# Attention scores by pairs of heads on partition halves, with one copy of k, in a Trainium2 encoder layer

## The chip, the cores and the metric

The kernel runs on one core of one Trainium2 chip. The metric is the device time in microseconds (us) of one execution, lower is better. The kernel before takes 1902.78 us, the median of 3 runs (1901.52 to 1905.02).

Five engines work from queues of their own: PE (TensorE, the matrix engine, whose weight loads the profile lists apart as PEld), DVE (VectorE), ACT (ScalarE), POOL (GpSimd) and SP (SyncE, which here only issues transfers). Each takes its instructions in the order of its queue, and waits on semaphores for the others.

## What is computed

The reference is one encoder layer, applied to two sequences of 1024 positions of width 1024 (16 tiles of 128 positions in all). Cut to the part that the change touches:

```python
def windowed_gqa(q, k, v, q_gain, k_gain, sink, rel_table):   # 8 heads of 64, 2 kv heads, GROUP = 4
    q = rms_norm(q.reshape(B, S, N_KV, GROUP, HEAD_DIM), q_gain)
    k = rms_norm(k.reshape(B, S, N_KV, HEAD_DIM), k_gain)
    ...                                     # kband, vband: the 3 blocks of 128 keys around a block of queries
    scores = jnp.einsum("bnqkgd,bnskd->bnkgqs", qb, kband).astype(jnp.float32)
    scores = scores * (1.0 / math.sqrt(HEAD_DIM))
    scores = jnp.where(mask[None, :, None, None], scores + bias[None, None], NEG)
    m = jnp.maximum(jnp.max(scores, axis=-1, keepdims=True), s_sink)
    e = jnp.exp(scores - m)
    probs = e / (jnp.sum(e, axis=-1, keepdims=True) + jnp.exp(s_sink - m))
    out = jnp.einsum("bnkgqs,bnskd->bnqkgd", probs.astype(v.dtype), vband)

def encoder_layer(...):
    h = rms_norm(x, norm1); proj = h @ w_in           # q, k, v and the gMLP halves gu, gv
    a = rms_norm(windowed_gqa(q, k, v, ...), attn_out_gain)
    g = rms_norm(chunked_spatial_gating(gu, gv, v_gain, w_s, b_s), gmlp_out_gain)
    x = x + jnp.concatenate([a, g], axis=-1) @ w_o
    h2 = rms_norm(x, norm2)
    return x + (jax.nn.silu(h2 @ w_gate) * (h2 @ w_up)) @ w_down
```

Query heads 0 to 3 use kv head 0, heads 4 to 7 use kv head 1. The inputs and outputs are float32.

## The kernel before

**Precision.** Each product is made from a high and a low part of both operands: high by high, high by low and low by high, three matmuls that add up in one PSUM bank (`mm3`, lines 221 to 225). ACT writes the high part of an operand, DVE the low part (the operand minus its high part).

**Stages.** The program loads and splits weights and makes the projections of tiles 0 to 3. Then comes the attention stage: for each of the 16 tiles, projection, normalisation of q and k, scores, softmax, product with v. After it come the gMLP part, the output projection, and the feed-forward part, which takes up most of the span.

**One tile in the attention stage**, by the names of the code:

- `proj_pieces` and `proj_evac` (lines 321 to 351): 24 matmuls of 512 columns make q (`pq`), 24 of 256 columns make k and v (`pkv`); ACT writes them to `qk` and `v`.
- `qk_sum`, `qk_scale` (353 to 373): DVE sums squares by head, POOL takes the power -1/2 (`qk_r`), and DVE multiplies. k is scaled by an instruction of its own (line 366), which also writes each of the two k heads twice, side by side; q is scaled by line 373.
- `qk_turn` (375 to 383): PE transposes two blocks of k (`pk`, one for each kv head, its two copies giving the two partition halves) and four of q (`pt`, two heads each).
- `qk_hi`, `qk_lo` (385 to 410): ACT writes the high parts, two of k (line 389) and two of q (394, each on 64 partitions); DVE the low parts, two of k (402) and two of q (408). In `qt` a head has its high part on its own partition half and its low part on the other half, and k stands on both halves of its tile.
- `Attn.scores(h)` (424 to 444): with that layout two matmuls over 128 rows do the work of a head (four partial products): `qt` by the high part of k, then by the low part. DVE then adds the bias and takes the minimum of a row (the signs are turned; line 435). Keys are 384 for 12 of the 16 tiles, and 256 for the first and last of each sequence. The results go to the four banks of the pool `xx`.
- `exps`, `norm`, `norm2` (446 to 475): ACT takes the exponentials, and DVE makes the factor of a row from the row's sum and the sink, with small instructions on 8 columns (lines 463 to 465, 471 to 475).
- `turn`, `turn_dma` (477 to 491): DVE or ACT writes the high half-precision part `ph` of the probabilities, POOL the low part (482), and SP issues one transposing transfer for a pair of heads into `pT`.
- `pv(h)` (493 to 504): nine matmuls of 64 columns for a head with 384 keys, into `po`.
- `finish`, `finish_pow`, `finish2` (506 to 523): DVE multiplies by the factor, ACT sums squares, POOL takes a power (`a_r`), DVE multiplies once more (line 522), and SP stores the tile.

**What sets the order.** A list of events gives each of these steps of each tile a time from the table `AT` (8 units to a tile), so that the projection of one tile, the scores of another and the product with v of a third are interleaved. The events are sorted and written out. The build's scheduler orders the queues from that, and POOL's queue is kept as written.

**Buffers.** Pools of 4 KB buffers in SBUF go by tags (line 87): 8 of tag M hold `sc`, `ph` and `pT`; 12 of tag L hold the k and v of both sequences (four k buffers and one of v for each) and `o`; 9 of tag S hold `qk`, `qt` and pieces of x.

Of the kernel before, what the change touches and what calls it, by code (L numbers as in the profile page):

```python
# [16 lines left out]
P = 128  # L17
# [3 lines left out]
TS = 8  # L21
# [7 lines left out]
NEG = -1e30  # L29
SQRT_2_PI = math.sqrt(2.0 / math.pi)  # L30
# [24 lines left out]
def kernel(  # L55
# [92 lines left out]
    nsk = cp.tile([P, NH], F32, name="nsk")  # L148
    nc.vector.tensor_scalar_mul(nsk, sks, -1.0)
# [155 lines left out]
    isv = cp.tile([P, 1], F32, name="isv")  # L305
    nc.gpsimd.tensor_tensor(sv, vtot, nhalf[:, :1], ALU.pow)
    nc.gpsimd.tensor_tensor(isv, vtot, pm[:, 1:2], ALU.pow)
    nc.vector.tensor_scalar_mul(sv, sv, 512.0)
    nc.vector.tensor_scalar_mul(isv, isv, 1.0 / 512.0)
# [4 lines left out]
    def seq_tiles(s):  # L314
        kT[s] = [[k4("L", f"k{c}{s}_{v}", (P, TS * P), F32R) for v in range(NKV)] for c in "hl"]
        vS[s] = k4("L", f"v{s}", (P, TS, 2, P), F16)
# [4 lines left out]
    def proj_pieces(t):  # L321
# [9 lines left out]
        nc.scalar.mul(qk[:, 0:AW], pq, r1)  # L331
# [31 lines left out]
    def qk_scale(t):  # L363
        qk, rqk = live[t]
        kd = qk[:, 640:896].rearrange("p (v c d) -> p v c d", v=NKV, c=2)
        nc.vector.tensor_tensor(
            kd,
            qk[:, AW : AW + P].rearrange("p (v d) -> p v d", v=NKV)[:, :, None, :].to_broadcast([P, NKV, 2, HD]),
            rqk[:, 8:10][:, :, None, None].to_broadcast([P, NKV, 2, HD]),
            ALU.mult,  # L370
        )
        qd = qk[:, 0:AW].rearrange("p (h d) -> p h d", h=NH)
        nc.vector.tensor_tensor(qd, qd, rqk[:, 0:8][:, :, None].to_broadcast([P, NH, HD]), ALU.mult)

    def qk_turn(t):
        qk = live[t][0]
        pk = mm(f"pk{t}", [P, NKV, P])
        for v in range(NKV):
            nc.tensor.transpose(pk[:, v, :], qk[:, 640 + v * P : 640 + (v + 1) * P], ident)
        pt = mm(f"pt{t}", [P, NH // 2, P])  # L380
        for j in range(NH // 2):
            nc.tensor.transpose(pt[:, j, :], qk[:, j * P : (j + 1) * P], ident)
        live[t] = (pk, pt)

    def qk_hi(t):
        s, i = divmod(t, TS)
        pk, pt = live[t]
        for v in range(NKV):
            nc.scalar.mul(kT[s][0][v][:, i * P : (i + 1) * P], pk[:, v, :], kgs)
        qt = k4("S", f"qt{t}", (P, NH, P), F32R)  # L390
        pairs = qt.rearrange("p (a b) t -> p a b t", b=2)
        for b in range(2):
            rows = slice(b * HD, b * HD + HD)
            nc.scalar.mul(pairs[rows, :, b, :], pt[rows], qg8[rows])
        qT[t] = qt

    def qk_lo(t):
        s, i = divmod(t, TS)
        pk, pt = live.pop(t)
        for v in range(NKV):  # L400
            ks = slice(i * P, (i + 1) * P)
            nc.vector.scalar_tensor_tensor(
                kT[s][1][v][:, ks], pk[:, v, :], kgs, kT[s][0][v][:, ks].bitcast(F32), ALU.mult, ALU.subtract
            )
        pairs = qT[t].rearrange("p (a b) t -> p a b t", b=2)
        for b in range(2):
            rows, other = slice(b * HD, b * HD + HD), slice((1 - b) * HD, (2 - b) * HD)
            nc.vector.scalar_tensor_tensor(
                pairs[other, :, b, :], pt[rows], qg8[rows], pairs[rows, :, b, :].bitcast(F32), ALU.mult, ALU.subtract
            )  # L410

    class Attn:
# [11 lines left out]
        def scores(self, h):  # L424
            t, W = self.t, self.W
            hp, j = divmod(h, 2)
            if j == 0:
                self.prs[hp] = k4("M", f"sc{t}_{hp}", (P, 2, 384))
            sc = self.prs[hp]
            v = h // 4  # L430
            ps = xx(f"ps{t}_{h}", [P, 384])
            keys = slice(self.lo_b * P, self.lo_b * P + W)
            nc.tensor.matmul(ps[:, :W], qT[t][:, h, :], kT[self.s][0][v][:, keys], start=True, stop=False)
# [1085 lines left out]
```

## Time and profile before

| | |
|---|---|
| median of the runs | 1902.78 us (1901.52 to 1905.02) |
| the profiled execution | 1903.98 us, its span 1902.2 us |
| first scores to last product with v | 56 to 317 us of the span |
| busy in the span: PE, DVE, ACT, POOL | 1827.1, 1251.1, 1027.5, 223.5 us |
| busy from 0 to 56 us: PE, DVE, ACT, POOL | 45.87, 29.77, 33.51, 17.82 us |
| busy from 310 us to the end: PE, DVE, ACT, POOL | 1558.86, 987.85, 793.89, 58.01 us of 1592.20 |

The profile is one execution, slightly slower than the median. "Busy" is the time in which an engine's instructions run; PE's matmuls overlap, and their ends are modelled, so the step from the start of one matmul to the start of the next tells more about PE than its busy time. A row of instruction groups reads: line, engine, operation, output and inputs by the names of the code, shapes, count, then busy time in us and mean length in ns, then the engine's idle time just before them with what ended it. PEclk is the granted share of TensorE's clock, and the DMA share the mean busy share of the 16 DMA engines.

### The profile page before, as it was taken

The page shows a single profiled execution, that of the slowest core. Times are in us where ns is not written, and L with a number is a line of the kernel's source. Part 1 is how long each engine was busy: PE and PEld are TensorE (multiplying, and loading weights), DVE is VectorE, ACT ScalarE, POOL GpSimd, SP SyncE. Part 2 cuts the span into 40 slices and gives each one's busy share as a digit, 9 for nine tenths or more (in the row PEclk, how much of TensorE's full clock was granted, in tenths as well). Part 3 has the DMA queues.
Part 4 walks back from the last instruction along what each step waited for, and adds up shares of the span by engine and source line. Part 5 has one row for each costly group of instructions (what it writes and reads, how often), then busy time and mean ns, then how long its engine had stood idle before and what let it go on. Part 6 is the DMA issues. An engine that isn't in the chain of part 4 may idle for free.

```text
span 1902.2 us, 26114 instructions
## 1 busy us (share of the span) xinstructions
PE 1827.1 (96%) x9584; PEld 1006.5 (53%) x9584; DVE 1251.1 (66%) x2321; ACT 1027.5 (54%) x1930; POOL 223.5 (12%) x214
## 2 busy tenths in 40 slices
PE   8789988999899999999999999999999999999999
PEld 6677766878655444444444444444444444444444
DVE  4989997688776778545555556456456855654661
ACT  6677887776566785544445345345344453333340
POOL 3366653111100000000000000000000000000000
PEclk9899989999999999999999999999999999999999
DMA  7478898443376886223223133133164564333641
GB/s 239 109 164 174 169 201 227 156 144 111 100 233 211 290 271 215 103 105 117 88 106 116 69 115 106 64 119 106 45 207 168 188 228 133 112 110 100 221 144 44
DMA packets 216209, 282.05 MB, mean 148 GB/s; under 512 B 103283, under 2 KB 138099, under 8 KB 216081
## 3 DMA queue, kind: packets, MB, share of 16 engines
q1 hardware_dynamic: 215632, 280.02, 48.3%
q8 instruction: 75, 1.23, 0.3%
q14 instruction: 54, 0.43, 0.1%
q0 software_dynamic: 304, 0.10, 0.0%
q10 hardware_dynamic: 144, 0.26, 0.0%
HBM read 177.04 MB, written 80.23 MB: 135 GB/s over the span
## 4 chain that ended last, share of the span: by engine, by line
PE 58%; DVE 2%; DMA 2%; issue 2%; ACT 1%; POOL 0%; POOLq 0%; SPq 0%; DVEq 0%
PE pd L1356 7%; PE pd L1358 7%; PE pd L1357 7%; PE pd L1082 4%; PE pd L1084 4%; PE pd L1083 4%; PE pa L1083 4%; PE pa L1082 4%; PE pa L1084 4%; PE pc L1082 4%; PE pc L1084 4%; PE pc L1083 4%; PE pb L1082 2%; PE pb L1083 2%; PE pb L1084 2%
## 5 line engine op out<-in xcount | busy, mean ns | idle before, releaser
L1356 PE MATMUL pd<-wop,a 128*128 128x512 f16 x616 | 233.5, 379 | 2.5 <-ACT a L117 2.5
L1357 PE MATMUL pd<-wop,a 128*128 128x512 f16 x616 | 233.5, 379 | 0.0
L1358 PE MATMUL pd<-wop,a 128*128 128x512 f16 x616 | 233.3, 379 | 0.0
L1083 PEld LDWEIGHTS <-op 128*128 128x128 f16 x1232 | 120.7, 98 | 149.2 <-issue 7.3
L1082 PEld LDWEIGHTS <-op 128*128 128x128 f16 x1232 | 122.5, 99 | 143.5 <-issue 1.0
L1084 PEld LDWEIGHTS <-op 128*128 128x128 f16 x1232 | 120.7, 98 | 146.8 <-issue 2.0
L1082 PE MATMUL pa<-top,op 128*128 128x512 f16 x352 | 133.4, 379 | 0.6 <-ACT ua L1200 0.6
L1084 PE MATMUL pa<-top,op 128*128 128x512 f16 x352 | 133.4, 379 | 0.0
L1083 PE MATMUL pa<-top,op 128*128 128x512 f16 x352 | 133.4, 379 | 0.0
L117 ACT ACTIVATE wop<-wd,wdr_r 128x512 f16<-128x512 f32 x66 | 47.3, 720 | 153.4 <-PE pd L1358 150.5
L117 ACT ACTIVATE a<-as,asr_r 128x512 f16<-128x512 f32 x154 | 102.2, 709 | 33.3 <-DMA as<-act_d 13.5
L482 POOL TENSOR_TENSOR ph<-sc,ph 128x768 f16<-128x768 f32 (+1 forms) x64 | 107.6, 1682 | 88.0 <-DVE ph L481 64.9
L118 DVE SCALAR_TENSOR_TENSOR wop<-wd,wdr_r,wop 128x512 f16<-128x512 f32 x66 | 49.2, 749 | 100.0 <-ACT wop L117 100.0
L118 DVE SCALAR_TENSOR_TENSOR a<-as,asr_r,a 128x512 f16<-128x512 f32 x154 | 108.8, 746 | 7.2 <-ACT a L117 6.9
L1211 ACT COPY ub<-pc 128x512 f32<-128x512 f32 x44 | 25.8, 585 | 160.0 <-PE pc L1084 160.0
L1356 PEld LDWEIGHTS <-a 128*128 128x128 f16 x616 | 60.4, 98 | 75.8 <-ACT a L117 3.4
L1358 PEld LDWEIGHTS <-a 128*128 128x128 f16 x616 | 60.3, 98 | 73.0 <-DVE a L118 0.7
L1357 PEld LDWEIGHTS <-a 128*128 128x128 f16 x616 | 60.3, 98 | 72.2
L451 ACT ACTIVATE sc<-sc,mx 128x384 f32<-128x384 f32 (+1 forms) x128 | 74.7, 584 | 26.4 <-DVE mx L435 25.6
L1025 ACT ACTIVATE junk_e<-g 128x1024 f32<-128x1024 f32 x44 | 46.4, 1054 | 75.9 <-DVE g L1195 75.9
L1217 DVE TENSOR_TENSOR ub<-ub,ua 128x512 f32<-128x512 f32 x44 | 30.4, 692 | 82.2 <-ACT ub L1211 82.2
L1192 ACT ACTIVATE g<-g,rs 128x512 f32<-128x512 f32 x57 | 41.1, 722 | 62.4 <-DVE g L1227 35.5
(381 smaller groups left out, 4806.9 us busy)
## 6 DMA issues: line engine op xcount, KB each, us to landing
as<-act_d SPq DMA_DIRECT2D x77, 512.0 KB, 3.7
act_d<-g SPq DMA_DIRECT2D x66, 256.0 KB, 2.0
xs<-in_xT_dram SPq DMA_DIRECT2D x28, 512.0 KB, 4.6
tr<-t_d SPq DMA_DIRECT2D x28, 512.0 KB, 5.4
raw<-in_wg_dram SPq DMA_DIRECT2D x24, 512.0 KB, 3.8
raw<-in_wu_dram SPq DMA_DIRECT2D x24, 512.0 KB, 4.2
act_d<-sa SPq DMA_DIRECT2D x44, 256.0 KB, 2.6
act_d<-sb SPq DMA_DIRECT2D x44, 256.0 KB, 2.9
```

Source lines behind the costliest of these rows:

```text
L117: nc.scalar.mul(hi, src, gain)
L118: nc.vector.scalar_tensor_tensor(lo, src, gain, hi, ALU.mult, ALU.subtract)
L451: nc.scalar.activation(sc[:, j, :W], sc[:, j, :W], AF.Exp, bias=self.mn[:, h : h + 1], scale=-1.0, accum_out=self.sums[:, h : h + 1],)
L482: nc.gpsimd.tensor_sub(ph[:, 1], sc[:, :, :W], ph[:, 0])
L1025: nc.scalar.activation(junk_e[0], src, AF.Square, accum_out=acc)
L1082: nc.tensor.matmul(ps, op[:, 0, k, :], th[:, k, :], start=first and k == 0, stop=False, **more)
L1083: nc.tensor.matmul(ps, op[:, 0, k, :], tl[:, k, :], start=False, stop=False, **more)
L1084: nc.tensor.matmul(ps, op[:, 1, k, :], th[:, k, :], start=False, stop=last and k == 3, **more)
L1192: nc.scalar.activation(dst, src, AF.Silu, scale=iv)
L1356: nc.tensor.matmul(ps, a[:, 0, s, cs], wop[:, 0], start=first and n == 0, stop=False, **kw)
L1357: nc.tensor.matmul(ps, a[:, 0, s, cs], wop[:, 1], start=False, stop=False, **kw)
L1358: nc.tensor.matmul(ps, a[:, 1, s, cs], wop[:, 0], start=False, stop=end, **kw)
```

## The change

Heads h and h+4, which have different kv heads, become a pair (`hp` from 0 to 3): head h on partitions 0 to 63, head h+4 on 64 to 127.

- q is written out of `pq` in the order of the pairs. k is scaled together with q by one DVE instruction, and is not copied; it is transposed once, both kv heads at a time, and its high and low parts are one instruction each. So are those of q, which are now two separate halves of `qt`.
- A pair's scores are six matmuls over 64 rows each, by turns on the lower and the upper partition half: three partial products (high by high, high by low, low by high) for each of the two heads. Both heads' scores are issued at one event, half a unit after the even head's and half a unit before the odd head's.
- The row factor takes two small DVE instructions in `norm` (for three) and two in `norm2` (for four); the scale of v goes into the constant that is added before the last normalisation.
- The last multiplication of a tile (`finish2`) goes from DVE to ACT.
- `pT` of every other pair lies in a buffer of tag L, where k's second copies (two buffers for each sequence) are no longer held.

```diff
     def qk_scale(t):
         qk, rqk = live[t]
-        kd = qk[:, 640:896].rearrange("p (v c d) -> p v c d", v=NKV, c=2)
-        nc.vector.tensor_tensor(
-            kd,
-            qk[:, AW : AW + P].rearrange("p (v d) -> p v d", v=NKV)[:, :, None, :].to_broadcast([P, NKV, 2, HD]),
-            rqk[:, 8:10][:, :, None, None].to_broadcast([P, NKV, 2, HD]),
-            ALU.mult,
-        )
-        qd = qk[:, 0:AW].rearrange("p (h d) -> p h d", h=NH)
-        nc.vector.tensor_tensor(qd, qd, rqk[:, 0:8][:, :, None].to_broadcast([P, NH, HD]), ALU.mult)
+        qd = qk[:, 0:640].rearrange("p (h d) -> p h d", d=HD)
+        nc.vector.tensor_tensor(qd, qd, rqk[:, :, None].to_broadcast([P, 10, HD]), ALU.mult)
...
     def qk_turn(t):
         qk = live[t][0]
-        pk = mm(f"pk{t}", [P, NKV, P])
-        for v in range(NKV):
-            nc.tensor.transpose(pk[:, v, :], qk[:, 640 + v * P : 640 + (v + 1) * P], ident)
+        pk = mm(f"pk{t}", [P, P])
+        nc.tensor.transpose(pk, qk[:, AW:640], ident)
...
     def qk_hi(t):
-        for v in range(NKV):
-            nc.scalar.mul(kT[s][0][v][:, i * P : (i + 1) * P], pk[:, v, :], kgs)
-        qt = k4("S", f"qt{t}", (P, NH, P), F32R)
...
+        nc.scalar.mul(kT[s][0][:, i * P : (i + 1) * P], pk, kgs)
+        qT[t] = k4("S", f"qt{t}", (P, 2, NH // 2, P), F32R)
+        nc.scalar.mul(qT[t][:, 0], pt, qg8)
...
     def qk_lo(t):
...
+        nc.vector.scalar_tensor_tensor(
+            kT[s][1][:, ks], pk, kgs, kT[s][0][:, ks].bitcast(F32), ALU.mult, ALU.subtract
+        )
+        nc.vector.scalar_tensor_tensor(
+            qT[t][:, 1], pt, qg8, qT[t][:, 0].bitcast(F32), ALU.mult, ALU.subtract
+        )
...
-        def scores(self, h):
+        def scores(self, hp):
...
-            nc.tensor.matmul(ps[:, :W], qT[t][:, h, :], kT[self.s][0][v][:, keys], start=True, stop=False)
-            nc.tensor.matmul(ps[:, :W], qT[t][:, h, :], kT[self.s][1][v][:, keys], start=False, stop=True)
...
+            ps = [xx(f"ps{t}_{hp}_{v}", [P, 384]) for v in range(NKV)]
+            for n, (a, b) in enumerate(((0, 0), (0, 1), (1, 0))):
+                for v in range(NKV):
+                    rows = slice(v * HD, (v + 1) * HD)
+                    nc.tensor.matmul(
+                        ps[v][:, :W], qT[t][rows, a, hp, :], kT[self.s][b][rows, keys], start=n == 0, stop=n == 2
+                    )
...
         def norm(self):
...
+            self.e = e = small("ab", NH)
+            nc.vector.tensor_tensor(e, self.mn, skc, ALU.min)
+            nc.vector.tensor_add(e, e, sks)
+            nc.scalar.activation(e, e, AF.Exp)
 
         def norm2(self):
...
+            self.f = small("f", NH)
+            nc.vector.tensor_add(self.e, self.sums, self.e)
+            nc.vector.reciprocal(self.f, self.e)
...
-            pT = k4("M", f"pT{self.t}_{hp}", (P, 2, 2, W), F16)
+            pT = k4("L" if hp % 2 else "M", f"pT{self.t}_{hp}", (P, 2, 2, W), F16)
...
         def finish_pow(self):
-            self.ra = rsqrt_mean("a", self.ms, 1, EPS, MIX_UP)
+            t = small("a_e", 1)
+            nc.vector.scalar_tensor_tensor(t, self.ms, MIX_UP**-2, epsv, ALU.mult, ALU.add)
+            self.ra = small("a_r", 1)
+            nc.gpsimd.tensor_tensor(self.ra, t, nhalf[:, :1], ALU.pow)
 
         def finish2(self):
             o = self.o
-            nc.vector.tensor_scalar_mul(o[:, 0], o[:, 0], self.ra)
+            nc.scalar.mul(o[:, 0], o[:, 0], self.ra)
...
         for h in range(NH):
-            at(T + A + h + AT["sc"], lambda t, h: att[t].scores(h), t, h)
-            at(T + A + 8 + h + AT["pv"], lambda t, h: att[t].pv(h), t, h)
+            at(T + A + 8 + h + AT["pv"], lambda t, h: att[t].pv(h % 2 * GROUP + h // 2), t, h)
             if h % 2:
+                at(T + A + h - 0.5 + AT["sc"], lambda t, h: att[t].scores(h // 2), t, h)
```

How the queues move shows at three places of tile 6. On PE before, a head's two score matmuls (`ps6_1` is the second head) stand alone between a product with v (`po4`) and pieces of a projection (`pq9`):

```order
L504 MATMUL po4_1783<-v0_417,pT4_3_1881 128x64
L433 MATMUL ps6_1_2027<-kh0_0_413,qt6_1620 128x384
L434 MATMUL ps6_1_2027<-kl0_0_415,qt6_1620 128x384
L223 MATMUL pq9_2014<-wq_hi_176,xh9_1776 128x512
L224 MATMUL pq9_2014<-wq_lo_177,xh9_1776 128x512
```

On PE of the change, the six of a pair (`ps6_1_0` and `ps6_1_1` are the two heads of pair 1) stand between pieces of the same projection:

```order
L226 MATMUL pq9_1990<-wq_hi_176,xl9_1772 128x512
L421 MATMUL ps6_1_0_2041<-kh0_414,qt6_1589 128x384
L421 MATMUL ps6_1_1_2042<-kh0_414,qt6_1589 128x384
L421 MATMUL ps6_1_0_2041<-kl0_415,qt6_1589 128x384
L421 MATMUL ps6_1_1_2042<-kl0_415,qt6_1589 128x384
L421 MATMUL ps6_1_0_2041<-kh0_414,qt6_1589 128x384
L421 MATMUL ps6_1_1_2042<-kh0_414,qt6_1589 128x384
L224 MATMUL pq9_1990<-wq_hi_176,xh9_1751 128x512
```

Two pairs of matmuls of two heads have become six in a row that change the partition half at each step. On DVE before, between the output of tile 4 (`o4`) and the last small instruction of its row factor (`f`):

```order
L508 TENSOR_TENSOR o4_2056<-po4_1783,f_1825 128x512
L435 ISA sc6_1_2051,mx_1991<-ps6_2_2052,bias_398 128x384
L435 ISA mx_1991 128x1
L471 TENSOR_TENSOR den_2079<-sums_1734,ab_1978 128x8
L366 TENSOR_TENSOR qk8_1891<-qk8_1891,qk_r_1989 128x256
L472 TENSOR_TENSOR den_2079<-den_2079,ab_1978 128x8
L156 TENSOR_SCALAR a_e_2069<-a_ms_2058 128x1
L373 TENSOR_TENSOR qk8_1891<-qk8_1891,qk_r_1989 128x512
L473 RECIPROCAL den_2079<-den_2079 128x8
L335 TENSOR_TENSOR rs_2152<-rstd_all_175,sv_407 128x1
L522 TENSOR_SCALAR o4_2056<-o4_2056,a_r_2071 128x512
L475 SCALAR_TENSOR_TENSOR f_2083<-ab_1978,isv_408,den_2079 128x8
```

On DVE of the change, at the same place:

```order
L493 TENSOR_TENSOR o4_2023<-po4_1758,f_1802 128x512
L459 TENSOR_TENSOR ab_1950<-sums_1707,ab_1950 128x8
L372 TENSOR_TENSOR qk8_1867<-qk8_1867,qk_r_1959 128x640
L460 RECIPROCAL f_2057<-ab_1950 128x8
L341 TENSOR_TENSOR rs_2125<-rstd_all_175,sv_407 128x1
L219 TENSOR_SCALAR x_e_2202<-x_ms_2072 128x1
L504 SCALAR_TENSOR_TENSOR a_e_2036<-a_ms_2025,epsv_408 128x1
```

The two scalings (lines 366 and 373) are one of 640 columns, two of the small instructions are gone, and the multiplication by `a_r` (line 522) has left the queue. It stands in ACT's queue now, as line 510, between the high part of k and that of q of tile 8:

```order
L442 ACTIVATE sc6_1_2040,sums_1962<-sc6_1_2040,mx_1961 128x384 x2
L386 ACTIVATE kh1_1450<-pk8_2079,kgs_91 128x128
L510 ACTIVATE o4_2023<-o4_2023,a_r_2038 128x512
L388 ACTIVATE qt8_2099<-pt8_2081,qg8_101 128x512
L333 ACTIVATE qk9_2122<-pq9_1990,rstd_all_175 128x2x4x64
```

POOL's queue has the same rows in the same order as before, but for one power at the start that is gone.

More of the change, by code (lines that the diff above doesn't have):

```diff
@@ L29 @@
 NEG = -1e30
+SINK_CLAMP = 80.0
 SQRT_2_PI = math.sqrt(2.0 / math.pi)
@@ L399, in qk_lo @@
         pk, pt = live.pop(t)
[L400 to L410, printed above, removed]
+        ks = slice(i * P, (i + 1) * P)
+        nc.vector.scalar_tensor_tensor(
[4 more added lines that the diff above has]
+        )
     class Attn:
```

77 lines of the change are left out of this document (31 added, 46 removed).

## The prediction

> **What bounds the kernel now.** I read the windows first, to find the stage that the change touches and the engine that is full there. The columns are the length, then the busy time of PE, PEld, DVE, ACT and POOL, the granted clock, the DMA share and GB/s:
>
> ```profile
> core 0: us, PE busy (x) PEld busy (x) DVE busy (x) ACT busy (x) POOL busy (x), PEclk, DMA share, GB/s
> 56.00:310.00 254.00, 222.34 (x1995) 178.47 (x1994) 233.50 (x616) 200.06 (x494) 147.63 (x102) 0.95 0.80 168
> ```
>
> In the attention stage DVE works for 233.50 of 254 us, 92%. PE's 222.34 holds the overlap of its matmuls; its own pace comes below. After 310 us nothing of attention is left but the last products with v, so whatever the stage gains or loses moves the end by as much. The next view is what PE waited for within the same window (total us, times, longest):
>
> ```profile
> PE ps L433 <- DVE mx L435: 7.4, 6, 2.3
> PE po L502 <- DMA pT<-ph: 6.3, 9, 1.4
> PE pk L379 <- DVE qk L366: 4.2, 4, 1.4
> PE pkv L223 <- DVE kl L402: 4.0, 5, 1.0
> PE pk L379 <- DVE den L472: 2.6, 2, 1.8
> PE pt L382 <- DVE rs L335: 2.3, 4, 0.8
> PE pk L379 <- DVE a_e L156: 1.9, 3, 1.3
> PE pt L382 <- DVE a_e L156: 1.0, 4, 0.3
> PE pt L382 <- DVE den L473: 1.0, 3, 0.4
> ...
> PE pt L382 <- DVE den L471: 0.2, 1, 0.2
> ```
>
> All but the DMA row name DVE: 7.4 + 4.2 + 4.0 + 2.6 + 2.3 + 1.9 + 1.0 + 1.0 + 0.2 = 24.6 us, and nearly all of these lines are ones that the change thins out. So the stage is bound by DVE, with PE close behind.
>
> **DVE.** The rows by shape, from 40 to 340 us (busy us, mean ns):
>
> ```profile
> L408 DVE SCALAR_TENSOR_TENSOR qt<-pt,qg,qt 64x512 fp32r<-64x512 f32 x32 | 24.0, 750 | 0.9
> L522 DVE TENSOR_SCALAR o<-o,a_r 128x512 f32<-128x512 f32 x16 | 21.9, 1371 | 4.5 <-POOL a_r L158 4.4
> L366 DVE TENSOR_TENSOR qk<-qk,qk_r 128x256 f32<-128x256 f32 x15 | 20.6, 1372 | 6.4 <-POOL qk_r L158 6.3
> L373 DVE TENSOR_TENSOR qk<-qk,qk_r 128x512 f32<-128x512 f32 x16 | 11.7, 734 | 0.0
> L402 DVE SCALAR_TENSOR_TENSOR kl<-pk,kgs,kh 128x128 fp32r<-128x128 f32 x32 | 9.7, 339 | 0.0
> L463 DVE TENSOR_TENSOR m<-mx,nsk 128x8 f32<-128x8 f32 x16 | 9.6, 600 | 0.0
> L464 DVE TENSOR_TENSOR ab<-m,mx 128x8 f32<-128x8 f32 x16 | 6.8, 424 | 0.0
> L475 DVE SCALAR_TENSOR_TENSOR f<-ab,isv,den 128x8 f32<-128x8 f32 x16 | 6.5, 406 | 0.0
> L472 DVE TENSOR_TENSOR den<-den,ab 128x8 f32<-128x8 f32 x16 | 4.5, 279 | 0.0
> ```
>
> Line 522 leaves DVE: 21.9 us. The low parts are half as many at the same length (512 and 128 columns on 128 partitions; a row's length does not tell 64 partitions from 128 here): 12.0 + 4.8 = 16.8. The small instructions 464, 472 and 475 go: 6.8 + 4.5 + 6.5 = 17.8.
>
> The two scalings become one of 640 columns. What it costs hangs on why line 366 takes 1372 ns for 256 columns where line 373 takes 734 for 512. The timeline tells:
>
> ```profile
> 86.95 1.64 POOL L482 TENSOR_TENSOR ph<-sc,ph 128x768 f16<-128x768 f32 x1
> 87.02 1.85 DVE L366 TENSOR_TENSOR qk<-qk,qk_r 128x256 f32<-128x256 f32 x1 [0.46 <-POOL qk_r L158]
> 88.87 0.68 DVE L373 TENSOR_TENSOR qk<-qk,qk_r 128x512 f32<-128x512 f32 x1
> ```
>
> ```profile
> L366 DVE TENSOR_TENSOR qk<-qk,qk_r x16: 414/1856/1930, 39.1 to 274.0; 128x256 f32<-128x256 f32 x16
> ```
>
> Line 366 takes 0.41 us alone (the least of min/median/max), and here it stood until POOL's instruction, begun just before it, was over at 88.59. POOL's queue is unchanged, so the merged scaling, which also waits for `qk_r`, will stand there too. Alone it should take 0.68 + 128 columns at (0.68 - 0.41)/256 us = 0.82, with the same standing (1372 - 414 = 958 ns) 1.78 us, or 28.4 for 16; rows 366 and 373 hold 20.6 + 11.7 = 32.3. It saves 4, and 19 if it never stands. The small sum before the last power now reads two tensors and may stand in the same way: between 0 and 7 us, by line 463's 600 ns against about 150 for such an instruction alone; I take 1. The sum is 21.9 + 16.8 + 17.8 + 4 - 1 = 59.5 us, and DVE falls to some 174 of 254 us, 69%. Should some standing pass to another instruction where line 522 leaves, even 20 us more would leave DVE under the others. It stops being the bound.
>
> **ACT.** The high parts halve, and `finish2` comes:
>
> ```profile
> L394 ACT ACTIVATE qt<-pt,qg 64x512 fp32r<-64x512 f32 x32 | 21.9, 683 | 2.7 <-PE pt L382 2.2
> L515 ACT ACTIVATE o<-o 128x512 f32<-128x512 f32 x16 | 10.0, 625 | 1.9 <-DVE o L508 1.8
> L389 ACT ACTIVATE kh<-pk,kgs 128x128 fp32r<-128x128 f32 x32 | 9.9, 358 | 7.2 <-PE pk L379 7.2
> ```
>
> That is -10.9 - 5.0 + 10.0, so ACT keeps about 194 of its 200 us. What is added is a wait: `finish2` stands in ACT's queue behind `a_r`, and behind it the high part of q and the next tile's evacuation of `pq`. DVE waited 4.4 us for `a_r` there. ACT has 54 us idle in the stage, so I cost it at nothing; without that cover it is those 4.4.
>
> **PE.** Of each tile one transpose goes: 16 times about 0.1 us (the four `pt` transposes below start at 206.42, the next matmul at 206.81) is 1.6. The scores are the open price. PE's timeline shows the steps:
>
> ```profile
> 181.34 0.36 PE L433 MATMUL ps<-kh,qt 128*128 128x256 f32 x1
> 181.55 0.28 PE L434 MATMUL ps<-kl,qt 128*128 128x256 f32 x1
> 181.67 0.28 PE L223 MATMUL pkv<-wkv,xh 128*128 128x256 f32 x1
> 181.79 0.28 PE L224 MATMUL pkv<-wkv,xh 128*128 128x256 f32 x1
> ...
> 202.64 0.42 PE L433 MATMUL ps<-kh,qt 128*128 128x384 f32 x1
> 202.90 0.34 PE L434 MATMUL ps<-kl,qt 128*128 128x384 f32 x1
> 203.08 0.39 PE L223 MATMUL pq<-wq_hi,xh 128*128 128x512 f32 x1
> ...
> 206.42 0.63 PE L382 MATMUL pt<-ident,qk 128*128 128x128 f32 x4 [0.25 <-DVE den L473]
> 206.81 0.47 PE L223 MATMUL pq<-wq_hi,xh 128*128 128x512 f32 x1
> ```
>
> A head with 384 keys costs 0.26 + 0.18 = 0.44 us, one with 256 keys 0.21 + 0.12 = 0.33; 0.08 of each is the start of the first. For 48 pairs of 0.88 and 16 of 0.66 that is 52.8 us. Now a pair is six matmuls over 64 rows, and no row of this profile shows matmuls on two partition halves. The bounds:
>
> - Both halves run at once: three steps, 3 x 0.18 + 0.08 = 0.62 and 3 x 0.12 + 0.08 = 0.44; 48 x 0.62 + 16 x 0.44 = 36.8 us, 16 less.
> - They run one after the other: 6 x 0.18 + 0.08 = 1.16 and 0.80; 55.7 + 12.8 = 68.5, 16 more.
> - They run one after the other, and the array empties at each change between whole matmuls and halves: a matmul of 256 columns lasts 0.28 and hands on after 0.12, so 0.16 for each emptying, twice for each of 64 pairs, 20.5 more on top.
>
> I take a value between: the streams overlap, but each matmul still loads its own weights, and steps of whole f32 matmuls hardly fall below 0.1, with 128 columns (0.39 for four) as with 256 (0.12). Six weight loads one after the other are 6 x 0.12 + 0.08 = 0.80 us a pair, 51.2 in all: 1.6 less than now. It lies nearest the rows that exist. A pair also needs two of the four banks at once; with DVE at 69% that costs nothing, and at most the 7.4 us of the row `ps` again.
>
> The Trainium skill, TensorEngine Tiling (Array Packing), section Tiling Modes, speaks against the change: changing the tiling mode, not just the tile, drains the engine. By that rule with my weight loads the two drains would take the 20.5 us back. No run here shows it yet. The same skill, TensorE: Matmul & The Clock Gate, Part 3, has matmuls on different row groups starting 4 ns apart and running together, which is the first bound.
>
> **The sum.** DVE thinned: of PE's 24.6 us of waits for it I take 20 back; the rest returns as waits for ACT, which writes the high part ahead of every low part. PE's own work: 1.6 + 1.6 = 3.2 back. Before the first scores DVE makes two low parts of k and two of q for tile 0, now one of each: about 1.1. The granted clock is 0.95 in the stage, and it falls where PE waits; with fewer waits I take 2 of the 12.7 us that 5% of the stage make. Against it, a faster stage meets the same 64 transposing transfers: the 6.3 us of waits for `pT` grow by, I say, 3. So 20 + 3.2 + 1.1 + 2 - 3 = 23.3 us: the profiled 1903.98 (a span of 1902.2 and 1.8 around it) becomes 1880.7, and the median of 1902.78 becomes **1879.5**.
>
> What is late next is PE itself, with the DMA engines (0.80 of 254 is 203 us of work) and ACT (194) close behind; that is why I do not take all of the waits. Buffers should not stop it: two of k's are given back in each sequence, and `pT` takes fewer than those.
>
> **The rivals.**
>
> - *Both halves at once.* Three steps a pair: 14.4 us less than mine, 1865. For it speaks only that the order alternates halves and banks at every step; against it, that weight loads already show in the step of 256 columns. 0.25.
> - *One after the other.* 17.3 us more PE work than mine, and PE is the bound then: 1897. For it: six matmuls of 384 columns cost what six do today. 0.10.
> - *Slower: one after the other, with emptying.* 17.3 + 20.5 = 37.8 on top of mine, 1917, at the scores on PE. It decides from 23.3 us, that is 0.36 us a pair over my 0.80. The profile has no such change of mode to look at. 0.09.
> - *The transfers bound the stage.* If 0.85 is all that the DMA engines give, 203 us need 239: a gain of 15, 1888. Against it: a share of 0.97 in the stage's end,
>
> ```profile
> 250.00:317.00 67.00, 53.50 (x517) 41.21 (x515) 58.40 (x150) 50.56 (x123) 35.06 (x25) 0.90 0.97 204
> ```
>
> where DVE (58.40 of 67) and transfers are both nearly full. 0.08.
>
> **How the numbers follow.** My case has the other 0.48. About 0.2%, 3.8 us, is what a measurement of this kernel can tell from no change. My case, the first rival and nearly all of the second and fourth end faster; the slower rival has 0.09; a mix near zero gets 0.04. The range goes from 1858, below the first rival by the 4.6 us of waits not counted and some clock, to 1898, just above the second, and leaves out the slower rival and the far tails.
>
> **What would show it.** In the changed kernel's profile DVE should be at 65 to 75% of the attention stage, and the waits of PE for DVE a quarter of 24.6. Line 372, the merged scaling, should take about 1.8 us with POOL's line 467 beside it. The six rows of line 421 should start about 0.12 us apart; pairs starting together mean the first rival, 0.18 apart the second, and a gap before and after the six the slower one. The forecast is wrong if the stage from first scores to last product with v is not 15 to 40 us shorter than 261, or if the time moves after 320 us, where nothing changes.

## The result, and the profile after

| | before | after |
|---|---|---|
| median, runs beside each other | 1902.15 us (1901.07 to 1905.02, 4 runs) | 1915.72 us (1913.46 to 1922.0, 4 runs) |
| the profiled execution, its span | 1903.98, 1902.2 us | 1922.0, 1920.1 us |
| first matmul of `pgu`, the first row after the stage | 307.3 us | 321.3 us |

The change is slower: a ratio of 1.0074, 95% interval 1.0046 to 1.0102, some 14 us where 23 less were forecast. `pgu` begins 14.0 us later: they are lost in the attention stage. (The profiled execution is the slowest of the four, and loses 4 us more behind it, where nothing was changed; its mean clock is 0.982, that of before 0.99.) The windows of the changed kernel, in the columns of the prediction (length, busy time of PE, PEld, DVE, ACT and POOL, clock, DMA share, GB/s): the same window, and its last part:

```profile
56.00:310.00 254.00, 223.76 (x2045) 165.03 (x2043) 185.27 (x501) 180.76 (x459) 137.67 (x99) 0.93 0.72 158
```

```profile
250.00:317.00 67.00, 52.70 (x525) 38.78 (x524) 52.57 (x133) 47.68 (x123) 39.12 (x26) 0.83 0.81 168
```

DVE is at 185.27 us, 73% of the window, inside the 65 to 75% that was forecast. No engine is full, and the transfers are at 0.72. The clock is lower, 0.83 in the last part against 0.90. What PE waited for (total us, times, longest):

```profile
PE pk L377 <- DVE rs L341: 16.3, 10, 2.9
PE po L487 <- DMA pT<-ph: 5.2, 8, 1.9
PE ps L421 <- DVE mx L426: 3.4, 1, 3.4
PE pkv L224 <- DVE kl L394: 2.4, 1, 2.4
PE pk L377 <- DVE qk L372: 1.9, 1, 1.9
PE pq L226 <- DVE xl L194: 1.0, 1, 1.0
```

Rows naming DVE make 25.0 us; they were 24.6. But they moved: 18.2 us stand at one place, the transpose `pk`, 0.3 to 2.9 us in each of 11 tiles. The name `rs` is only the DVE instruction that ended last before; what `pk` needs is the scaled k of line 372. The DVE rows from 40 to 340 us:

```profile
L372 DVE TENSOR_TENSOR qk<-qk,qk_r 128x640 f32<-128x640 f32 x15 | 27.2, 1812 | 15.8 <-POOL qk_r L159 15.8
L454 DVE TENSOR_TENSOR ab<-ab,sks 128x8 f32<-128x8 f32 x16 | 17.4, 1086 | 0.0
L397 DVE SCALAR_TENSOR_TENSOR qt<-pt,qg,qt 128x512 fp32r<-128x512 f32 x16 | 12.0, 750 | 5.8 <-ACT qt L388 5.8
L394 DVE SCALAR_TENSOR_TENSOR kl<-pk,kgs,kh 128x128 fp32r<-128x128 f32 x16 | 5.6, 349 | 16.9 <-ACT kh L386 16.9
```

and the one line for line 372 alone (least, median, most ns):

```profile
L372 DVE TENSOR_TENSOR qk<-qk,qk_r x16: 814/2250/2270, 39.1 to 283.0; 128x640 f32<-128x640 f32 x16
```

The low parts cost what was forecast. The merged scaling takes 0.81 us alone, 2.25 in the median and 1.81 in the mean. Line 454, one of the two small instructions that the change left in `norm`, takes 1.09 us for 8 columns. The timeline of one tile shows both:

```profile
150.74 1.66 POOL L467 TENSOR_TENSOR ph<-sc,ph 128x768 f16<-128x768 f32 x1 [3.02 <-DVE ab L453]
150.86 1.56 DVE L454 TENSOR_TENSOR ab<-ab,sks 128x8 f32<-128x8 f32 x1
152.34 0.81 DVE L366 TENSOR_REDUCE qk_ss<-sq 128x10 f32<-128x640 f32 x1
153.55 0.16 DVE L157 TENSOR_SCALAR qk_e<-qk_ss 128x10 f32<-128x10 f32 x1
153.79 1.96 POOL L159 TENSOR_TENSOR qk_r<-qk_e,nhalf 128x10 f32<-128x10 f32 x1 [0.88 <-DVE qk_e L157]
155.72 1.64 POOL L467 TENSOR_TENSOR ph<-sc,ph 128x768 f16<-128x768 f32 x1
155.78 2.26 DVE L372 TENSOR_TENSOR qk<-qk,qk_r 128x640 f32<-128x640 f32 x1 [0.93 <-POOL qk_r L159]
158.19 0.30 PE L377 MATMUL pk<-ident,qk 128*128 128x128 f32 x1 [1.75 <-DVE rs L341]
```

Twice in a tile DVE stands until a POOL instruction begun just before is over: at line 454 behind the low part of one pair, ahead of the sum `qk_ss`; and at line 372 behind the low part of the next, which follows `qk_r` in POOL's queue. Both stand on one path: sum, power, scaling, transpose. PE is there 1.75 us early. (To "stand" is said here of an instruction that is much longer than its least length, while another engine's runs.)

On PE, the six matmuls of a pair (x2 stands for two that begin together):

```profile
201.59 0.39 PE L225 MATMUL pq<-wq_lo,xh 128*128 128x512 f32 x1
201.81 0.40 PE L226 MATMUL pq<-wq_hi,xl 128*128 128x512 f32 x1
202.14 0.44 PE L421 MATMUL ps<-kh,qt 64*128 64x384 f32 x2
202.42 0.33 PE L421 MATMUL ps<-kl,qt 64*128 64x384 f32 x2
202.59 0.34 PE L421 MATMUL ps<-kh,qt 64*128 64x384 f32 x2
202.86 0.50 PE L224 MATMUL pq<-wq_hi,xh 128*128 128x512 f32 x1
203.20 0.39 PE L225 MATMUL pq<-wq_lo,xh 128*128 128x512 f32 x1
```

The two halves do run together: three steps, not six. But the step into the group is 0.33 us where a whole matmul of 512 columns steps by 0.22, the first step inside it 0.28 against 0.17, the step out of it 0.27 against 0.17, the next 0.34 against 0.23: about 0.1 us too much four times. A pair costs PE 0.72 us from its first matmul to the next other one, and some 0.2 more on the two neighbours: 0.92, where two heads took 0.88.

**The 14 us, added up.** From 56 us to the first `pgu` (251.3 us before, 265.3 after), PE has no matmul running for 30.4 and 33.5 us: 3.1 more. The trace has the clock at half for 23.9 and 37.5 us, 4.3 and 6.4 of them in that idle time. Half of what is left of such a stretch is lost to PE's work: 9.8 and 15.6 us, 5.8 more. The remainder, about 5 us, is PE's own work at full clock, 211.1 and 216.3 us. It goes with the scores: counted from the first score to the first `pgu`, it lies between 215.4 and 217.3 us in the traces of all kernels below with the row-tiled scores, and between 208.3 and 211.1 in all with the old ones, however long PE was idle. So PE's idle time did not shrink by 20; it grew by 3.

### The profile page after: what moved, and what is told of

It is laid out like the page before. It is cut to its first block, busy times and chain, and to the rows that moved or that the text cites. A ratio compares the mean times of both kernels' runs of the same rounds, so it can differ in the third digit from the quotient of the medians.

```text
span 1920.1 us, 26190 instructions
## 1 busy us (share of the span) xinstructions
PE 1844.7 (96%) x9696; PEld 1003.1 (52%) x9696; DVE 1207.4 (63%) x2211; ACT 1017.5 (53%) x1914; POOL 218.0 (11%) x213
## 4 chain that ended last, share of the span: by engine, by line
PE 57%; DVE 2%; DMA 2%; issue 2%; ACT 1%; POOL 0%; POOLq 0%; DVEq 0%; ACTq 0%
PE pd L1344 7%; PE pd L1346 7%; PE pd L1345 7%; PE pa L1070 4%; PE pd L1070 4%; PE pa L1071 4%; PE pa L1072 4%; PE pd L1072 3%; PE pd L1071 3%; PE pc L1070 3%; PE pc L1071 3%; PE pc L1072 3%; PE pb L1070 2%; PE pb L1071 2%; PE pb L1072 2%
## 5 line engine op out<-in xcount | busy, mean ns | idle before, releaser
L1205 DVE TENSOR_TENSOR ub<-ub,ua 128x512 f32<-128x512 f32 x44 | 30.4, 691 | 82.0 <-ACT ub L1199 79.6
L426 DVE CUSTOM_DVE_ANT_0 sc<-ps,bias 128x384 f32<-128x384 f32 (+1 forms) x128 | 62.5, 515 | 20.6 <-issue 9.9
```

Of the source, the lines that this page charges most:

```text
L426: nc.vector.tensor_tensor_reduce(out=sc[:, v, :W], in0=ps[v][:, :W], in1=bias[:, h, self.off : self.off + W], scale=1.0, scalar=-NEG, op0= ...
```

## The experiments

I began with three theories. **A**: the pace is set by a chain through the queues in each tile (end of `pkv`, ACT's evacuation, DVE's `qk_ss`, POOL's `qk_r`, DVE's scaling, PE's `pk`, the high and low parts, the next `pkv`), and what counts of DVE is the length of that chain, not the sum of its work. **B**: DVE's load sets the pace, and something else in the change, the scores, costs what the thinner DVE saves. **C**: `finish2` on ACT, waiting for `a_r`, holds up ACT's queue. Ratios are to the kernel before, run on the same chip, with a 95% interval.

### The parts of the change apart

**e1**: the scores, the copies of k and the scalings of before, with the change's `norm`, `norm2`, `finish_pow` and `finish2`.

```diff
-        nc.vector.tensor_tensor(qd, qd, rqk[:, :, None].to_broadcast([P, 10, HD]), ALU.mult)
+        nc.vector.tensor_tensor(kd, ..., rqk[:, 8:10]..., ALU.mult)   # and qd, scores, qk_turn, qk_hi, qk_lo as before
```

> The kernel before with only the shorter row factor (two small DVE instructions for three, two for four) and the last multiplication on ACT; scores, k's two copies and the pair of scalings as before. Theory A (PE stands at the transposes of k until the chain of sums, power and scaling is through, whatever DVE's load): DVE loses some 40 us of work, PE still waits 15 to 25 us for it, and the time stays within 5 us of before, 1897 to 1905. Theory B (the thinner DVE does give its waits back, and the change loses them again to the passages of PE between whole matmuls and halves): without those passages the gain shows, 1880 to 1890.

It took 1905.06 us, at the very end of A's range, ratio 1.0021 (1.0010 to 1.0032), with this window:

```profile
56.00:310.00 254.00, 224.04 (x1987) 181.20 (x1986) 210.34 (x555) 203.23 (x499) 145.87 (x101) 0.95 0.77 168
```

DVE has 23 us less to do than before (210.34 against 233.50, where A had said some 40), and the time is not shorter but a little longer. B falls, and with it the first term of the prediction.

**e2**: the rest of the change without these, that is the row-tiled scores and one copy of k alone.

```diff
-            nc.vector.tensor_tensor(e, self.mn, skc, ALU.min)
-            nc.vector.tensor_add(e, e, sks)
+            m = small("m", NH)      # norm, norm2, finish_pow and finish2 (on DVE) as before
```

> The change without the shorter row factor and with the last multiplication on DVE, so pairs on partition halves, one copy of k and one scaling alone. Theory A: PE's pace is 4 to 5 us dearer, the waits at the transposes stay, and DVE's small instructions add little: 1912 to 1922, no faster than the change. Theory B: the passages without the relief, 1920 to 1930.

1922.71 us, 1.0109 (1.0096 to 1.0122): in B's range and 0.7 us above A's, so this run alone does not speak against B; e1 does. The scores with one k cost 21 us here, and the thinner normalisation gave some 7 of them back.

**e3**: only `finish2` back on DVE.

```diff
-            nc.scalar.mul(o[:, 0], o[:, 0], self.ra)
+            nc.vector.tensor_scalar_mul(o[:, 0], o[:, 0], self.ra)
```

> The change with the last multiplication of a tile back on DVE. Theory A: it stands in the chain of neither k nor q for long: within 4 us of the change (1912 to 1920). Rival C (the wait for the power, now in ACT's queue ahead of the high part of q, is what holds the tile up): 8 us or more faster, 1900 to 1908.

1914.17 us, 1.0063 (1.0050 to 1.0075): the change's own time. C falls.

**e8**: only the buffers of `pT` as before.

```diff
-            pT = k4("L" if hp % 2 else "M", f"pT{self.t}_{hp}", (P, 2, 2, W), F16)
+            pT = k4("M", f"pT{self.t}_{hp}", (P, 2, 2, W), F16)
```

> The change, but all transposed probabilities lie in the M buffers, as before (the freed buffers of k's other copy stay unused). It prices the third part of the change by itself. Theory A: the transfers into pT are not what bounds; PE's waits for pT (8.5 us with the change, 6.3 before) grow by a few us: 1914-1922. If the buffers had hurt (other banks of memory, transfers that start earlier and collide), the time falls to 1905-1912.

1914.65 us, 1.0063 (1.0051 to 1.0075). Half of `pT` in k's old buffers is worth nothing, either way.

**e6**: the six matmuls head after head.

```diff
-            for n, (a, b) in enumerate(((0, 0), (0, 1), (1, 0))):
-                for v in range(NKV):
+            for v in range(NKV):
+                for n, (a, b) in enumerate(((0, 0), (0, 1), (1, 0))):
```

> The change, but the six matmuls of a pair are issued head after head (three on the lower half of the partitions, then three on the upper), so that almost nothing can run together. A pair should then take some 0.5 us more on PE (six steps of 0.174 in place of three), 32 us in all. If PE's work set the pace of the stage, the time grows by all of it: 1945-1950. Theory A (the pace is a chain in which PE has 2-3 us of idle time per tile at the transposes): the pairs that stand between the end of pkv and pk lie in that idle time, and a third to two thirds of the 32 us show: 1926-1938.

1914.49 us, 1.0059 (1.0041 to 1.0077): no difference that these runs can tell, and both forecasts missed, because their premise did. PE's timeline:

```profile
203.28 0.45 PE L421 MATMUL ps<-kh,qt 64*128 64x384 f32 x2
203.56 0.34 PE L421 MATMUL ps<-kl,qt 64*128 64x384 f32 x2
203.74 0.34 PE L421 MATMUL ps<-kh,qt 64*128 64x384 f32 x2
```

Issued three and three, the matmuls of the two halves still begin together and in three steps. So the price of the overlap was not measured; that the order within a group of six does not matter was.

### The standing beside POOL

**e4**: all low parts of the probabilities on DVE.

```diff
-            nc.gpsimd.tensor_sub(ph[:, 1], sc[:, :, :W], ph[:, 0])
+            nc.vector.tensor_sub(ph[:, 1], sc[:, :, :W], ph[:, 0])
```

> The change with the low part of the probabilities made by DVE and not by POOL, so that POOL has only its powers left and nothing of DVE stands behind it. DVE gets 64 instructions of about 0.85 us more and loses what it stands. Theory A: the scaling falls from 2.26 to about 0.82 us, each wait of PE at the transposes gets 1.4 us shorter, 12 tiles make 12 to 17 us: 1896 to 1905. Theory B: no change in the passages and DVE at over 80%: 1913 to 1925.

1900.97 us, 0.9997 (0.9989 to 1.0006): 14 us better than the change, with 21 us more work on DVE (206.53 us in the window). The theory that DVE's work is what costs has the wrong sign. Neither the scaling nor line 454 stands any more: 0.82 and 0.16 us in the mean.

**e5**: only the third pair's low part, the one that follows `qk_r`, on DVE; POOL keeps the other 48.

```diff
+            (nc.vector if hp == 2 else nc.gpsimd).tensor_sub(ph[:, 1], sc[:, :, :W], ph[:, 0])
```

> The change, but the low part of the probabilities goes from POOL to DVE for the third pair of each tile alone: the instruction that follows qk_r in POOL's queue and beside which the merged scaling stands (2.26 us instead of 0.82). The other 48 stay on POOL. Theory A (a chain per tile from the end of pkv over the power and the scaling to the transposes and the next pkv sets the pace, and the standing lengthens it by 1.4 us in some 11 tiles): scaling at 0.82-1.0 us, and most of the 15 us that the move of all 64 gave: 1902-1908. Rival D (that move helped because POOL, its 64 hops and the shared port were relieved in general): a quarter of it, 1911-1916.

1898.93 us, 0.9989 (0.9977 to 1.0000), faster than even A had it. One POOL instruction a tile out of the way gives all that moving four gave, and D falls. (The third pair's transfer could start earlier too, but PE's waits for `pT` hardly change, 8.5 to 7.7 us from 56 to 330 us.) The scaling no more stands (DVE's row from 56 to 310 us), and PE's waits at `pk` go from 18.2 to 6.3:

```profile
L372 DVE TENSOR_TENSOR qk<-qk,qk_r 128x640 f32<-128x640 f32 x13 | 10.7, 822 | 4.6 <-POOL qk_r L159 4.0
```

```profile
PE pk L377 <- DVE qk L372: 4.0, 5, 1.3
PE pk L377 <- ACT o L500: 2.3, 3, 1.5
```

**e11**: e4 with the power computed twice. The order of every other engine's queue is the same as in e4.

```diff
-        nc.gpsimd.tensor_tensor(r, t, nhalf[:, :w], ALU.pow)
+        for _ in range(2 if name == "qk" else 1): nc.gpsimd.tensor_tensor(r, t, nhalf[:, :w], ALU.pow)
```

> The change with all low parts on DVE (the kernel that ran 1901), and the power qk_r computed twice, one after the other, on POOL, which is idle there 5/6 of the time; the order of the instructions on all other engines is the same, and nothing but the chain from qk_ss to the scaling becomes longer, by 1.96 us a tile. Theory A: PE waits for it at the transposes; 0.8-1.5 us of it show in each of some 11 to 13 tiles: 1910-1920. Rival D or any theory in which a load (PE, DVE, DMA) sets the pace: 1900-1904.

1916.16 us, 1.0077 (1.0059 to 1.0096): 15 us slower than e4. POOL is busy for 67 of 254 us, no other engine has more to do than in e4, and neither the scaling (0.83 us) nor line 454 stands; only one link of the chain is 1.96 us longer. PE's waits at `pk` go from 5.4 to 11.0 us (56 to 330 us):

```profile
PE pk L377 <- DVE a_e L504: 7.9, 5, 2.0
PE pk L377 <- DVE qk L372: 3.1, 3, 1.4
```

That is the most direct evidence that the chain's length counts. Two things in it are not as A had them. In e4 DVE came to the scaling some 1.1 us after the power was ready, so that only some 0.8 us a tile of the 1.96 reach the scaled k. And only 7.7 us of the loss come after the first scores; these begin at 61.6 us in place of 55.0, and ahead of them the powers of the first tiles begin every 6.2 us in place of 4.2.

**e9** and **e18**: the cure of e5 on e1, and on the kernel before alone.

> The kernel before with the change's part on the normalisation and finish2 on ACT (the kernel that ran 1905), and the low part of the third pair's probabilities on DVE in place of POOL. DVE then carries some 222 of 254 us. Theory A: the scalings stand no more beside POOL, the chain is 1 us shorter in some 11 tiles: 1893-1900, faster than before. Rival B (DVE's load sets the pace): 12 us more on DVE, 1906-1915. Rival D: 1902-1906.

> The kernel before with one edit alone: the low part of the third pair's probabilities on DVE. Its first scaling stands beside POOL for 1.1 us a tile too (1.52 us in place of 0.41), and DVE's busy time stays at some 231-234 of 254 us, for what it gains by not standing it pays with 16 more instructions of 0.88 us. Theory A: the chain is 1.1 us shorter at the same load: 1893-1899. Rival B (DVE's load sets the pace there): 1899-1904. Set beside the kernel of 1893, which has the same cure and some 15 us less work on DVE, it also tells what thinning DVE is worth once the chain is short: nothing by Theory A if both agree within 2 us.

e9 took 1893.47 us, 0.9955 (0.9939 to 0.9971), and e18 1896.01, 0.9961 (0.9947 to 0.9975). Their windows, e9 and e18:

```profile
56.00:310.00 254.00, 229.46 (x2063) 186.26 (x2062) 217.06 (x582) 210.97 (x515) 125.23 (x88) 0.96 0.82 179
```

```profile
56.00:310.00 254.00, 226.07 (x2030) 182.58 (x2028) 229.87 (x640) 202.13 (x499) 125.24 (x87) 0.96 0.81 176
```

With 229.87 us on DVE, 90% of the window, the kernel before gets the gain from one line; thinning DVE by 13 us on top is within the intervals of nothing.

### How the chain reaches the end

**e15**: the transposes later in PE's queue.

```diff
-    qksum=-16.06, scale=-12.784, turnq=-12.228, hi=-11.568, ...
+    qksum=-16.06, scale=-12.784, turnq=-11.228, hi=-10.968, ...
```

> The change with nothing but two numbers of the schedule raised by one (turnq and hi): PE's transposes pk and pt stand behind one more pair of scores and some eight more steps of pq, about 2.5 us of work; POOL, DVE's instructions and their standing stay. Theory A (PE waits at the transposes because the chain from pkv to the scaling is longer than the work queued ahead of them): the scaling still takes 2.2 us, PE's 18 us of waits at pk fall under 8, and the time to 1900-1909; what could eat it is that pk and pt hold their banks later, so that DVE's low parts and the next pkv wait. Rival E (the standing costs because DVE itself loses the time, wherever PE stands): 1911-1917.

1914.01 us, 1.0058 (1.0041 to 1.0074). A's forecast missed, and E's was met. PE's waits at `pk` nearly vanished, and came back elsewhere: `po` on `pT`, from 8.5 us (56 to 330 us) to

```profile
PE po L487 <- DMA pT<-ph: 24.2, 20, 3.3
```

Where they came from, one tile in the timeline:

```profile
155.45 0.82 ACT L466 CAST ph<-sc 128x768 f16<-128x768 f32 x1
156.67 1.96 POOL L159 TENSOR_TENSOR qk_r<-qk_e,nhalf 128x10 f32<-128x10 f32 x1 [0.88 <-DVE qk_e L157]
158.60 1.65 POOL L467 TENSOR_TENSOR ph<-sc,ph 128x768 f16<-128x768 f32 x1
160.28 0.83 ACT L466 CAST ph<-sc 128x768 f16<-128x768 f32 x1 [1.73 <-POOL ph L467]
163.97 0.20 PE L487 MATMUL po<-v,pT 128*128 128x64 f16 x1 [1.60 <-DMA pT<-ph]
```

The third pair's high part is written at 156.27, but its low part begins at 158.60, behind `qk_r` in POOL's queue; ACT's next high part waits for it, its transfer lands 3.7 us after it ends, and PE waits there. So two paths to PE run through the same place in POOL's queue, and with one out of the way the other was as long. That left open whether the chain's length counts (**A′**, wherever PE stands) or the time for which DVE's queue stands still (**E**). Two kernels tell them apart:

**e20**: `norm=7.642` becomes `norm=8.2`, which puts line 454 behind `qk_ss`; the scaling goes on standing.

> The change with one number of the schedule raised (norm by 0.56): the two small operations of the normalisation that the change made stand behind qk_ss in DVE's queue and no more ahead of it, where the second took 1.08 us in the mean and up to 1.6, standing beside POOL's low part. Theory A' (the latency from pkv to the scaling counts, wherever PE stands): qk_ss comes up to 1.4 us earlier in some 10 tiles, 1902-1909. Theory E (what counts is how long DVE's queue stands still): the small operation stands just as long in its new place, or DVE waits that much longer for qk_r: 1911-1917.

**e21**: `qksum=-16.06` becomes `qksum=-15.2`, which puts `qk_r` behind that low part in POOL's queue; the standing goes, but the chain begins later.

> The change with one number of the schedule raised (qksum by 0.86): in POOL's queue the power qk_r stands behind the low part of the third pair and no more ahead of it. The low part comes 2 us earlier and the scaling has no POOL instruction to stand beside (0.82 us in place of 2.26). But qk_ss and qk_r come later, by 1 to 2 us, so that the chain from pkv to the end of the scaling is about as long as before. Theory A': 1911-1919. Theory E: DVE's queue is free for 1.4 us a tile more, 1899-1907.

e20 took 1906.01 us, 1.0032 (1.0016 to 1.0047); e21 1914.0, 1.0081 (1.0066 to 1.0096). Both fall where A′ had them, and neither where E had it. Lines 372 and 454 in e20 and in e21:

```profile
L372 DVE TENSOR_TENSOR qk<-qk,qk_r 128x640 f32<-128x640 f32 x13 | 24.6, 1892 | 9.5 <-POOL qk_r L159 9.5
L454 DVE TENSOR_TENSOR ab<-ab,sks 128x8 f32<-128x8 f32 x16 | 8.2, 513 | 0.0
```

```profile
L372 DVE TENSOR_TENSOR qk<-qk,qk_r 128x640 f32<-128x640 f32 x13 | 13.5, 1038 | 14.9 <-POOL qk_r L159 14.9
L454 DVE TENSOR_TENSOR ab<-ab,sks 128x8 f32<-128x8 f32 x16 | 18.7, 1166 | 0.0
```

In e20 the scaling stands for nearly as long as in the change, and the kernel is 5 to 8 us faster (5 to 6 by the ratios of e3, e6 and e8, which run at the change's level, 8 by the change's own). Line 454 stands less there, 0.51 us in place of 1.08, so DVE's queue stands still for less in e20 too, and e20 alone does not separate the theories. e21 does: lines 372, 453 and 454 take 34.7 us there from 56 to 310 us, 39.4 in e20 and 44.2 in the change, so DVE's queue stands still for least, and nothing is won. (An edit of the schedule or of the engine also makes the build's scheduler order a few instructions of other queues anew, in e5 and e20 too; e11 is free of that.)

The same trend runs through all kernels. From the traces, in the mean of tiles 4 to 14: the time from the end of the last matmul of `pkv` to the end of the instruction that scales k, and the time from one tile's `pk` to the next.

| kernel | to the scaled k, us | a tile, us |
|---|---|---|
| e22 (below) | 6.7 | 15.7 |
| e9 | 7.2 | 15.5 |
| e18 | 7.3 | 15.6 |
| e16 (below) | 7.5 | 16.0 |
| e23 (below) | 7.6 | 15.5 |
| before | 8.1 | 16.5 |
| e5 | 8.2 | 16.0 |
| e1 | 8.6 | 16.5 |
| e20 | 8.8 | 16.5 |
| e4 | 8.8 | 16.3 |
| e3 | 9.3 | 17.4 |
| **the change** | 9.3 | 17.4 |
| e21, e6, e8, e2, e15 | 9.5 each | 17.4, 17.5, 17.3, 18.0, 17.4 |
| e11 | 9.6 | 17.0 |

From the five shortest (7.2 and 15.7 in the mean) to the eight longest (9.5 and 17.4), a microsecond on the chain is 0.8 on the tile. The rule is not exact: e11 has the longest chain and 17.0 us, and before and e5 differ by 0.5 us a tile at nearly the same chain.

### The fastest forms

**e16**: e9 with e15's two numbers.

> The fastest kernel so far (old scores, the change's normalisation, low part of the third pair on DVE; 1893), with the same two numbers raised by one. PE waits there 7.6 us at the transposes (pk and pt) in all. Theory A: at most those come back, less what the later banks cost: 1888-1895.

1902.75 us, 0.9997 (0.9984 to 1.0011): a miss, 8 us slower than e9 by the ratios. The transposes already stood where they should: as in e15, the waits came back as waits for `pT`, 20.1 us in place of 8.3.

**e22** and **e23**: e9 and e5, each with e20's number.

> The kernel of 1893 (old scores, the change's normalisation, low part of the third pair on DVE), with norm raised by 0.56. There the small operations take 0.25 and 0.49 us, so that little stands. A': a few tenths of a us in some tiles, 1889-1894. E: 1892-1896.

> The change with the low part of the third pair on DVE (1899) and norm raised by 0.56; there the second small operation takes 1.03 us. A': up to 0.9 us earlier in some 10 tiles: 1891-1896. E: 1896-1901.

1891.50 us, 0.9959 (0.9944 to 0.9974), and 1892.09 us, 0.9961 (0.9947 to 0.9975), both in A′'s ranges and below E's. e23 is the change itself with one low part and one number moved: some 21 us faster than the change by the ratios, and faster than the kernel before. PE hardly waits in it at `pk` for the scaling (56 to 330 us):

```profile
PE po L487 <- DMA pT<-ph: 9.4, 11, 2.2
PE ps L421 <- DVE mx L426: 4.5, 1, 4.5
PE pkv L224 <- DVE kl L394: 2.0, 2, 1.6
PE pk L377 <- DVE qk L372: 1.5, 4, 0.5
```

But old scores with the same cure (e22), and before with half of it (e18), come out the same. The row-tiled scores, one copy of k and 42 us less on DVE buy nothing that these runs can tell; the cure is all of the gain. The traces of e23 and e22 show two effects that cancel: to the first `pgu` PE is idle for 19.2 us in e23 and 25.2 in e22, but its own work from the first score on is 217.1 us against 208.8.

## Why the prediction was wrong

- **The failed step** is in the sum: "DVE thinned: of PE's 24.6 us of waits for it I take 20 back." The thinning came (48 us less in the window, 73% of it, where 69% was forecast), and all of the waits stayed, 25.0 us. They were read as waits for a full engine, because DVE was at 92%. They were waits for the end of a chain in which DVE itself waits for POOL's 1.96 us and stands beside POOL's low parts; from the end of `pkv` to the scaled k it was 8.1 us and became 9.3. e1, e18 against e22, and e4 show that DVE's work was not what cost; e11, e5, and e20 with e21 show that the chain was.
- **The merged scaling** was forecast to stand, "1.78 us" in the mean, and takes 1.81 in the mean (2.25 once the stage runs): the size was right. What the forecast left out is what it holds up: before, k was scaled first, by an instruction of its own, and `pk` waited only for that one; now k comes with q. From the end of `qk_r` to the scaled k it was 1.75 us in the mean of tiles 4 to 14, and is 2.21.
- **The small instructions** were priced one by one as gone, and the only one feared was "the small sum before the last power", at 1 us. The one that stands is line 454, 17.4 us where line 453, as small, takes 2.5, and ahead of `qk_ss` on the chain. e20 prices its place there: 5 to 8 us.
- **The scores on PE** were forecast at 0.80 us a pair, and cost 0.92. The mechanism was rival 1, both halves at once, and the gaps of the slower rival came with it and ate it. The rule that changing the tiling mode drains the engine (the Trainium skill, TensorEngine Tiling (Array Packing), section Tiling Modes) agrees with the rows: about 0.4 us around each pair, 64 pairs, 26 us, where the prediction gave it 20.5; some of it is the start of the first matmul, which two heads paid as well (0.08 each). Overlap and gaps nearly cancel; where 3.2 us of PE's own work were forecast to go, 5 came.
- **The clock** was forecast to give 2 us back and took some 6.
- **The start** was forecast to give 1.1 us; the first scores begin at 56.2 us, before at 56.1.
- **ACT** worked 181 us of the window, where 194 were forecast, and `finish2` there costs nothing (e3). The waits for `pT` did not grow by 3 us but fell from 6.3 to 5.2, and the buffers did not matter (e8). That neither would bind held.
- **The slower rival** had the sign and, at 1917, nearly the time, but by luck: it had the halves run one after the other, where they overlap, and all of the loss in PE's scores, which explain some 5 of the 14 us.

Why the stage is 14 us longer is shown in its parts: 3 us of idle time, 6 of clock, 5 of work on PE. That a longer chain brings a lower clock with it is seen (e20, e5 and e23 have 20 to 21 us at half clock, the change 37.5), but not in proportion (e21 30.7, e15 34.1), and what exactly lets the clock fall was not tested; it stays open.

## What to carry to other kernels

A row "PE waits for DVE" beside a DVE at 92% does not say that DVE's load is the bound: follow what DVE waited for there, and ask what lengthens the path from the wait back to its start. Price an instruction not only by its own length, but by what it stands beside and what stands behind it; here one instruction on another engine, moved, was worth more than 42 us of work taken away. A cheap proof is to double a link of the suspected chain on an engine that is idle.

## What the runs showed of the hardware

- Two matmuls over 64 rows on different partition halves begin together (a median of 4 ns apart over 192 pairs in the changed kernel) and also when they are issued three and three (10 ns in e6). That they start so close is what the Trainium skill states (TensorE: Matmul & The Clock Gate, Part 3). In e6 the fourth matmul issued starts beside the first, so the order of issue within such a group made no difference.
- A group of such matmuls between whole ones costs about 0.1 us four times: on the step into it, on its first step, on the step out, and on the step after (the last not where a product with v follows).
- A DVE instruction with two inputs in SBUF (lines 372 and 454) stands until a POOL instruction begun just before it is over, however short its own work is: 0.16 us became 1.56, 0.82 became 2.26. The Trainium skill (SBUF — State Buffer, section SBUF: two separate sides) calls the shared port an exclusive lock held for the whole instruction; the rows agree.
- The traces have the clock at half in stretches of 3.4 us and multiples of it: 7 stretches in the changed kernel's stage, 3.4 to 13.7 us long, and 4 before, 3.4 to 10.2. PE's longest wait there was 3.4 us, before 2.3.
